# Reordering the joints of a two-layer SSD, Conformer and Fourier trunk: early products between layers, the gated norm inside the scan, and moved side work

## The chip, the cores and the metric

The kernel is one program on one core of a Trainium2 chip. The metric is the device time of one execution in microseconds (us). The kernel before takes 1757.48 us, the median of three runs (1753.33 to 1760.16).

## The reference

The program advances 640 tokens (128 of context, 512 of a noisy sample) through two layers in fp32. Layer 0 mixes tokens with a state-space scan and a convolution, layer 1 with a Fourier transform, and each layer ends in a feed-forward block with a 3x3 depthwise convolution. Before each block stands a norm that is scaled and shifted by `mod`, a product of the condition with `w_mod`. Cut to what matters:

```python
mod = silu(cond) @ w_mod[i] + b_mod[i]
sh1, sc1, gt1, sh2, sc2, gt2 = split(mod, 6)
hm = rmsnorm(x, g_mix[i]) * (1 + sc1) + sh1
if i % 2 == 0:
    proj = hm @ w_in                       # z, xbc, dt, glu
    y = ssd_scan(silu(conv5(xbc)), softplus(dt), ...)   # both directions, chunks of 128
    y_ssd = rmsnorm(y * silu(z), norm_g)   # the gated norm
    u = glu[..., :1024] * sigmoid(glu[..., 1024:])
    u = silu(layernorm(conv31(u)))
    out = concatenate([y_ssd, u]) @ w_out
else:
    out = fft2(hm by groups).real @ w + b
x = x + gt1 * out
hf = rmsnorm(x, g_ffn[i]) * (1 + sc2) + sh2
val, gate = split(conv3x3(hf @ w_up), 2)
x = x + gt2 * ((val * silu(gate)) @ w_down)
```

## The kernel before

Channels lie on the 128 partitions and the 640 tokens along the free axis, so an activation is 8 tiles of 128x640. Every large product is done as three products of fp32r halves: a weight tile `raw` arrives by SP's queue (L203), ScalarE rounds it to `wh` (L216), GpSimd subtracts to get `wl` (L219), and TensorE adds wh x xh, wh x xl and wl x xh in one accumulator (L227). The tokens are cut in two segments, in most places of 320 columns, so that a tile of eight k takes 24 matmuls for each segment.

The order on each engine is made by a scheduler of the tile framework, which places an instruction by its place in the program, the release of the buffers and the `issue_after` marks. An engine runs its queue strictly in that order, and so does SP with its DMAs.

The work comes in this order: the first norm with the `mod` columns that it needs; eight pairs of products of the convolution branch (each gives a tile of `u` at L855, a SiLU gate times a value) with `mod` vectors between them on VectorE (L268 twice and L272 for one of 128x1024); `time_steps` (L531 to L548), which makes the scan's step sizes; the projections and the scan of 4 groups by 5 chunks, with parts of products as fillers (the tables GATES, PROJ, LNAT, UFILL name the step of each); the gated norm (`y_segment`, its sums at L894 and L899, `apply` at L906 to L908); the product with `w_out`, first its u half and then its y half; feed-forward 0; the Fourier layer; feed-forward 1.

At a joint between two blocks, `by_segment` finishes the last product segment by segment: it adds to `x` (L354), collects squares (ScalarE L318, VectorE ssq L322), sums them over channels on TensorE (L329) and from this normalizes (hmt L340, xh L348, xl L349). `first_up` then starts three tiles of the next up-product together, k by k, on segment 0.

The layer norm of the convolution branch needs sums over channels. Within the convolution three GpSimd adds for each of 7 pieces make them (L631 to L633), and L950 to its neighbours apply them.

```python
UFILL = {19: 1, 20: 2, 21: 2}     # tiles of the u half as filler of the last scan steps
LNAT = (0, 1, 9, 10)              # scan steps of mean, centring, rstd, scaling
MODSP = (2, 2, 2, 2)              # mod vectors after each tile of the first projection
```

## Time and profile before

| | |
|---|---|
| Median of three runs | 1757.48 us |
| Profiled execution | 1752.11 us, span 1749.4 us |
| TensorE busy | 1642.1 us (94%) |
| VectorE busy | 1348.4 us (77%) |
| GpSimd busy | 825.4 us (47%) |
| ScalarE busy | 692.7 us (40%) |
| DMA | 189.20 MB, mean 108 GB/s |

Busy shares are means over stages with different limits. The windows of 25 us show where TensorE was full (25.00 of 25) and where it waited or ran at a lower granted clock; the list of waits says for whom it waited.

### The profile page before, as it was taken

What the parts mean: (1) busy time and instruction counts of PE and PEld (TensorE: products, weight loads), DVE (VectorE), ACT (ScalarE), POOL (GpSimd) and SP (SyncE); (2) the same over time, 40 slices, a digit from 0 to 9 for tenths busy, and PEclk for the clock granted to TensorE, in tenths of its full rate; (3) what the DMA queues carried; (4) which work ended last, traced back from release to release, by engine and by line L of the source; (5) the groups of instructions that cost most, each with busy time, mean ns of one, the idle gap of its engine ahead of it and who ended that gap; (6) DMA issues with size and microseconds to landing.
All of it is one profiled execution on the core that took longest, in us unless ns stands there. A gap on an engine that the chain in (4) does not pass through costs nothing.

```text
span 1749.4 us, 27932 instructions
## 1 busy us (share of the span) xinstructions
PE 1642.1 (94%) x10828; PEld 1576.8 (90%) x10828; DVE 1348.4 (77%) x2390; ACT 692.7 (40%) x1207; POOL 825.4 (47%) x556
## 2 busy tenths in 40 slices
PE   7989998999899879999999999889799999999997
PEld 4789987888799879999999999779799999999996
DVE  7688586878665387899999999885989838817846
ACT  4312225888763253332231232455533223313324
POOL 1233346554655353554465355404445635544544
PEclk9999998999999999999999999999999999999998
DMA  8446332332331342225324422432533232222123
GB/s 290 162 143 185 122 111 77 109 109 79 91 105 71 102 150 81 74 70 181 119 64 155 145 63 85 138 112 73 173 109 97 64 94 70 65 86 81 49 58 114
DMA packets 81911, 189.20 MB, mean 108 GB/s; under 512 B 7540, under 2 KB 33043, under 8 KB 81780
## 3 DMA queue, kind: packets, MB, share of 16 engines
q1 hardware_dynamic: 78836, 184.03, 33.7%
q10 hardware_dynamic: 2944, 3.41, 0.6%
q8 instruction: 85, 1.39, 0.3%
q14 instruction: 46, 0.38, 0.1%
HBM read 183.57 MB, written 3.83 MB: 107 GB/s over the span
## 4 chain that ended last, share of the span: by engine, by line
PE 54%; DVE 39%; issue 3%; ACT 2%; POOL 1%; DMA 1%; ACTq 0%; DVEq 0%; POOLq 0%
PE acc L227 46%; DVE cva L1039 12%; DVE mm L268 7%; DVE x L354 3%; DVE ssq L322 2%; DVE modc L272 2%; DVE cva L1028 2%; DVE hmt L340 2%; DVE mjunk L268 1%; PE misc L621 1%; PE misc L813 1%; PE misc L248 1%; PE acc L329 1%; DVE yT L906 1%; ACT sqt L318 1%
## 5 line engine op out<-in xcount | busy, mean ns | idle before, releaser
L219 POOL TENSOR_TENSOR wl<-raw,wh 128x512 fp32r<-128x512 f32 (+5 forms) x314 | 561.5, 1797 | 649.9 <-ACT wh L216 642.2
L227 PE MATMUL acc<-xh,wh 128*128 128x320 f32 (+2 forms) x2064 | 491.8, 315 | 12.1 <-DVE u L855 8.1
L1039 DVE SCALAR_TENSOR_TENSOR cva<-acc,cw,cva 128x441 f32<-128x441 f32 (+2 forms) x704 | 477.4, 691 | 16.2
L227 PE MATMUL acc<-xh,wl 128*128 128x320 f32 (+2 forms) x2064 | 485.5, 312 | 2.4 <-POOL wl L219 2.4
L227 PE MATMUL acc<-xl,wh 128*128 128x320 f32 (+2 forms) x2064 | 486.5, 313 | 0.2 <-DVE xl L349 0.2
L216 ACT CAST wh<-raw 128x512 fp32r<-128x512 f32 (+5 forms) x314 | 238.0, 768 | 576.5 <-PE acc L227 412.0
L227 PEld LDWEIGHTS acc<-xh,wh 128*128 128x128 f32 (+1 forms) x2064 | 352.6, 190 | 17.7 <-issue 14.7
L227 PEld LDWEIGHTS acc<-xl,wh 128*128 128x128 f32 (+1 forms) x2064 | 352.0, 190 | 2.4 <-issue 0.9
L227 PEld LDWEIGHTS acc<-xh,wl 128*128 128x128 f32 (+1 forms) x2064 | 350.8, 190 | 3.3 <-POOL wl L219 2.7
L354 DVE SCALAR_TENSOR_TENSOR x<-acc,modc,x 128x128 f32<-128x128 f32 (+2 forms) x240 | 112.0, 498 | 151.5 <-PE acc L227 147.0
L227 PE MATMUL acc<-fh,wh 128*128 128x320 f32 (+2 forms) x832 | 207.0, 311 | 5.3 <-DVE cva L1039 2.3
L227 PE MATMUL acc<-fh,wl 128*128 128x320 f32 (+2 forms) x832 | 206.6, 311 | 2.8 <-POOL wl L219 2.7
L227 PE MATMUL acc<-fl,wh 128*128 128x320 f32 (+2 forms) x832 | 206.2, 310 | 0.0
L227 PEld LDWEIGHTS acc<-fh,wh 128*128 128x128 f32 x832 | 143.7, 189 | 6.4 <-issue 6.0
L227 PEld LDWEIGHTS acc<-fh,wl 128*128 128x128 f32 x832 | 143.7, 189 | 4.6 <-POOL wl L219 4.2
L227 PEld LDWEIGHTS acc<-fl,wh 128*128 128x128 f32 x832 | 143.8, 189 | 0.6
L268 DVE SCALAR_TENSOR_TENSOR mm<-mm 128x1024 f32<-128x1024 f32 x72 | 126.9, 1763 | 0.8
L1067 POOL TENSOR_TENSOR cva<-cva 128x640 f32<-128x640 f32 x44 | 71.1, 1615 | 98.1 <-ACT cva L1066 98.1
L268 DVE SCALAR_TENSOR_TENSOR mjunk<-mraw,crow 128x1024 f32<-128x1024 f32 x68 | 97.7, 1437 | 6.9 <-DMA mraw<-in_w_modT 6.4
L1028 DVE SCALAR_TENSOR_TENSOR cva<-acc,cw,cva 128x127 f32<-128x127 f32 x176 | 60.0, 345 | 49.9 <-ACT cva L1024 46.2
L1071 POOL TENSOR_TENSOR fl<-cva,fh 128x640 fp32r<-128x640 f32 x44 | 70.8, 1608 | 31.8 <-ACT fh L1070 31.8
L1066 ACT ACTIVATE cva<-cva 128x640 f32<-128x640 f32 x44 | 32.4, 736 | 130.1 <-DVE cva L1039 130.1
(253 smaller groups left out, 1927.2 us busy)
## 6 DMA issues: line engine op xcount, KB each, us to landing
raw<-in_ffn_w_up SPq DMA_DIRECT2D x88, 512.0 KB, 3.7
raw<-in_w_in SPq DMA_DIRECT2D x40, 512.0 KB, 3.9
mm<-in_w_modT SPq DMA_DIRECT2D x36, 512.0 KB, 3.7
mraw<-in_w_modT SPq DMA_DIRECT2D x34, 512.0 KB, 3.8
e<-acsd SPq DMA_DIRECT2D x40, 256.0 KB, 3.4
raw<-in_ffn_w_down SPq DMA_DIRECT2D x32, 256.0 KB, 2.7
raw<-in_ffn_w_down SPq DMA_DIRECT2D x16, 448.0 KB, 3.4
raw<-in_w_out SPq DMA_DIRECT2D x24, 256.0 KB, 3.0
```

What stands on the lines that cost most here:

```text
L216: S.copy(wh[:, ks, :], raw[:, ks, :])
L219: G.tensor_tensor(wl[:, ks, :], raw[:, ks, :], wh[:, ks, :].bitcast(F32), op=SUB)
L227: PE.matmul(part(ps, s), lhsT=wt[:, k, :], rhs=tok(at, s), start=(k == 0 and p == 0), stop=(k == n - 1 and p == 2))
L268: V.scalar_tensor_tensor(junk, in0=raw[:, cs_], scalar=1.0, in1=crow[j][:, cs_], op0=MULT, op1=MULT, accum_out=m[:, 2 * o + j:2 * o + j + 1])
L272: V.tensor_scalar(modc[l][:, i, :], m[:, 0:2], b, None, op0=ADD)
L322: V.tensor_tensor(tok(self.a, s), tok(self.a, s), t, op=ADD)
L340: V.scalar_tensor_tensor(tok(t, sub), in0=tok(x[:, k, :], sub), scalar=a[:, k, j:j + 1], in1=flat(bc[:, o:o + size(sub)], sub), op0=MULT, ...
L354: last = V.scalar_tensor_tensor(tok(x[:, m, :], sub), in0=part(ps, s, o, sub), scalar=gt[:, m, j:j + 1], in1=tok(x[:, m, :], sub), op0=MUL ...
L1028: V.scalar_tensor_tensor(a[:, lo:hi], in0=ps[:, BASE + lo + d:BASE + hi + d], scalar=w(1, c), in1=a[:, lo:hi], op0=MULT, op1=ADD)
L1039: last = V.scalar_tensor_tensor(av[:, r0:r1, c0:c1], in0=pv[:, r0 + dr_:r1 + dr_, c0 + dc:c1 + dc], scalar=w(r, c), in1=av[:, r0:r1, c0:c1 ...
L1067: G.tensor_tensor(cv[0], cv[0], cv[1], op=MULT)
L1071: G.tensor_tensor(l_, cv[0], h_.bitcast(F32), op=SUB)
```

## The change

The edits, without what they are for:

1. `first_up` is split in `early(k)` and `rest`. At the joints w_out to feed-forward 0 and Fourier to feed-forward 1, the 72 matmuls of segment 0 of the next up-product are issued k by k: those of k 0 to 3 ahead of the second segment's sum of squares, those of k 4 to 7 behind it. At the joint of feed-forward 0 to the Fourier layer, `over_channels` does the same with 16 plain fp32 matmuls. Its table d1 is loaded at the front.
2. The gated norm's two segments are called inside the scan loop, after chunks 2 and 4 of the last group; `apply` stands ahead of all eight tiles of the u half, and its `yl` subtraction runs on VectorE instead of GpSimd.
3. `time_steps` is a generator in two parts, after u tiles 1 and 2, each issued behind u and tanh and ahead of the `mod` vectors.
4. The 21 GpSimd adds in the convolution become 7 adds of 128x640 at scan steps 0 and 1; the layer norm's steps move back by two.
5. Two of three groups of scale columns of the first norm are `mod` vectors on VectorE instead of TensorE products; `columns` does its transposes ahead of its adds.
6. The first three weight tiles are loaded ahead of the first `mod` loads on SP.
7. The `mod` vectors are spread anew: MODSP, MODS1, MODST, and five of them (MODSW) beside the u half of `w_out`.

```diff
-DTAT = 1
+DTAT = (1, 2)
-SCPE = (0, 3, 6)
+SCPE = (0,)
-MODSP = (2, 2, 2, 2)
+MODSP = (3, 3, 2, 0)
-LNAT = (0, 1, 9, 10)
+LNAT = (0, 2, 3, 11, 12)
-UFILL = {19: 1, 20: 2, 21: 2}
+MODSW = (1, 1, 1, 1, 1, 0, 0, 0)
-MODS1 = ({j: 1 for j in range(6)}, ((0,) * 8,) * 3)
+MODS1 = ({j: 1 for j in (0, 2, 4, 6, 7)}, ((0,) * 8,) * 3)
-MODST = (1, 0, 1, 0, 1, 0, 1, 0)
+MODST = (0,) * 8
...
             product(src, k0, acts, (s,), after)
+            if i:
+                for k in range(KD - NLAG):
+                    early(k)
             bc[i] = ss.finish(s, i * size(segs[0]))
         for k in range(KD - NLAG, KD):
             then(bc[0], segs[0], k)
+            early(k)
...
+        def early(k):
+            if k == 0:
+                ws.extend(weights(A["ffn_w_up"][l], b) for b in FIRST)
+                ps0.update((b, acc()) for b in FIRST)
+            for b, w in zip(FIRST, ws):
+                mtile_k(ps0[b], w, acts[k], k, KD, SEGS[:1])
...
+        first = [first_weights(A["w_dt"], 0), first_weights(w_in, 32), weights(w_in, 24)]
         mod_start(0)
...
+        with tc.issue_after(last.ins), tc.issue_after(tanh.ins):
+            if i in DTAT:
+                next(steps)
...
-                G.tensor_tensor(yl, y, yh.bitcast(F32), op=SUB)
+                V.tensor_tensor(yl, y, yh.bitcast(F32), op=SUB)
...
+    def ln_sum(i):
+        if i == 0:
+            L["sum"] = sm.tile([P, T], F32, tag="ssq", name="usum", bufs=1)
+        G.tensor_tensor(L["sum"], L["sum"] if i else u[:, 0, :], u[:, i + 1, :], op=ADD)
...
+            if g == 3 and c in (2, 4):
+                apply.append(y_segment(CHUNKED[c == 4]))
...
+    u_fill(len(utodo))
     for f in apply:
         f()
-    u_fill(len(utodo))
```

On TensorE, at the joint of w_out and feed-forward 0, the rows around the second segment's sum of squares (ssq, sqt against ones) and of the 16 fp32 products L1101, before (yh and yl are w_out's operands, xh and xl the next block's; 68 rows of the 72 products L227 are left out):

```order
L227 MATMUL acc<-yl,wh 128x320
L227 MATMUL acc<-yh,wl 128x320
L329 MATMUL acc<-ssq,ones 128x320
L329 MATMUL acc<-sqt,ones 128x320
L227 MATMUL acc<-xh,wh 128x320
L227 MATMUL acc<-xl,wh 128x320
...
L227 MATMUL acc<-xl,wh 128x320
L227 MATMUL acc<-xh,wl 128x320
L1101 MATMUL acc<-mraw,sc__85 2x128 x16
```

and now, around the same two matmuls:

```order
L229 MATMUL acc<-yl,wh 128x320
L229 MATMUL acc<-yh,wl 128x320
L229 MATMUL acc<-xh,wh 128x320
L229 MATMUL acc<-xl,wh 128x320
...
L229 MATMUL acc<-xl,wh 128x320
L229 MATMUL acc<-xh,wl 128x320
L331 MATMUL acc<-ssq,ones 128x320
L331 MATMUL acc<-sqt,ones 128x320
L229 MATMUL acc<-xh,wh 128x320
```

Thirty-six products of the next block now stand ahead of L331 and 36 behind it; before, all 72 stood behind L329.

On VectorE, around the third tile u (L855, now L913), the time steps (dtmp) and the `mod` vectors (mjunk), before:

```order
L540 TENSOR_TENSOR dtmp_820<-dtmp_820 128x160
L541 TENSOR_TENSOR dtmp_821<-dtmp_820 128x160
L542 TENSOR_SCALAR dtmp_821<-dtmp_821 128x160
L544 TENSOR_TENSOR dtmp_821<-dtmp_821 128x160
...
L855 SCALAR_TENSOR_TENSOR u<-sg,acc 128x128
L545 TENSOR_SCALAR dtmp_821<-dtmp_821 128x160
L855 SCALAR_TENSOR_TENSOR u<-sg,acc 128x512
```

and now:

```order
L270 SCALAR_TENSOR_TENSOR mjunk,mm<-mraw,crow_110 128x1024
L270 SCALAR_TENSOR_TENSOR mjunk,mm<-mraw,crow_111 128x1024
L274 TENSOR_SCALAR modc_88<-mm,vec 128x2
L913 SCALAR_TENSOR_TENSOR u<-sg,acc 128x128
L913 SCALAR_TENSOR_TENSOR u<-sg,acc 128x512
L603 TENSOR_SCALAR dtmp_792<-dtmp_792 128x160
L270 SCALAR_TENSOR_TENSOR mjunk,mm<-mraw,crow_110 128x1024
```

The chain of the time steps, which stood ahead of u, starts behind it.

On GpSimd, between the last weight splits of the convolution branch and the scan's first steps (usum holds the layer norm's sums, xdd and hd belong to the scan), before:

```order
L631 TENSOR_TENSOR cs<-u 128x4x67
L632 TENSOR_TENSOR cs<-cs 128x2x67
L633 TENSOR_TENSOR usum<-cs 128x67
L734 TENSOR_TENSOR xdd<-xb,dte 128x256 x7
L743 TENSOR_TENSOR hd<-h_2465,cdec 128x256
```

and now:

```order
L791 TENSOR_TENSOR xdd<-xb,dte 128x256 x2
L986 TENSOR_TENSOR usum<-usum,u 128x640
L791 TENSOR_TENSOR xdd<-xb,dte 128x256
L986 TENSOR_TENSOR usum<-usum,u 128x640
L791 TENSOR_TENSOR xdd<-xb,dte 128x256 x2
L986 TENSOR_TENSOR usum<-usum,u 128x640
L791 TENSOR_TENSOR xdd<-xb,dte 128x256
L986 TENSOR_TENSOR usum<-usum,u 128x640
L791 TENSOR_TENSOR xdd<-xb,dte 128x256
L800 TENSOR_TENSOR hd<-h_2430,cdec 128x256
```

The sums no longer stand ahead of all scan work; four of the seven adds stand among the first xdd.

## Rows read from the trace of the kernel before

**Rows 1.** The page, busy time of each engine over the span:

```profile
PE 1642.1 (94%) x10828; PEld 1576.8 (90%) x10828; DVE 1348.4 (77%) x2390; ACT 692.7 (40%) x1207; POOL 825.4 (47%) x556
```

**Rows 2.** What TensorE waited for: total us, times, longest us:

```profile
PE acc L329 <- DVE ssq L322: 25.7, 8, 7.5
PE acc L227 <- DVE x L354: 8.5, 2, 6.3
PE acc L227 <- DVE u L855: 8.1, 1, 8.1
...
PE acc L227 <- DVE cva L1039: 4.5, 4, 2.3
...
PE misc L717 <- ACT xb L719: 3.7, 1, 3.7
```

**Rows 3.** Windows: stretch, length, PE, PEld, DVE, ACT, POOL busy, granted clock, DMA:

```profile
725.00:750.00 25.00, 25.00 (x172) 25.00 (x171) 23.09 (x39) 8.05 (x10) 14.88 (x8) 1.00 0.22 62
1125.00:1150.00 25.00, 17.67 (x107) 13.46 (x107) 22.78 (x63) 14.03 (x28) 7.31 (x9) 0.86 0.69 236
1250.00:1275.00 25.00, 22.32 (x138) 19.97 (x139) 18.21 (x36) 12.41 (x23) 4.83 (x2) 0.86 0.49 170
1325.00:1350.00 25.00, 24.77 (x168) 24.53 (x167) 25.00 (x41) 8.04 (x11) 16.91 (x8) 1.00 0.31 90
```

**Rows 4.** Timeline at the front: start us, us, engine, line, names [idle before]:

```profile
19.10 8.08 POOL L219 TENSOR_TENSOR wl<-raw,wh 128x128 fp32r<-128x128 f32 x6 [18.66 <-ACT wh L216]
...
21.09 2.28 DVE L268 SCALAR_TENSOR_TENSOR mjunk<-rawv,crow 128x1024 f32<-128x1024 f32 x1
...
27.38 0.22 PE L255 MATMUL acc<-con,mrow 2*128 2x2 f32 x1 [3.17 <-DVE modc L256]
...
31.09 1.22 DVE L268 SCALAR_TENSOR_TENSOR mjunk<-rawv,crow 128x1024 f32<-128x1024 f32 x1
```

**Rows 5.** The chain of waits at the front, a group of mod columns on TensorE:

```profile
40.52 1.84 PE misc L248 x16
```

**Rows 6.** Timeline around u tile 2, TensorE:

```profile
99.77 0.46 PE L227 MATMUL acc<-xh,wl 128*128 128x320 f32 x2
...
113.71 0.87 PE L227 MATMUL acc<-xh,wh 128*128 128x320 f32 x2 [8.13 <-DVE u L855]
114.38 0.74 PE L227 MATMUL acc<-xl,wh 128*128 128x320 f32 x2
```

**Rows 7.** Timeline at the scan's start, ScalarE:

```profile
273.55 2.01 ACT L719 COPY xb<-misc 128x384 f32<-128x384 f32 x5 [7.40 <-POOL usum L633]
```

**Rows 8.** The page's costliest groups, a GpSimd add of 128x640: busy, mean ns, idle before:

```profile
L1067 POOL TENSOR_TENSOR cva<-cva 128x640 f32<-128x640 f32 x44 | 71.1, 1615 | 98.1 <-ACT cva L1066 98.1
```

**Rows 9.** Timeline of the gated norm on VectorE and TensorE:

```profile
518.89 1.01 DVE L896 TENSOR_TENSOR yT<-yT,gz 128x384 f32<-128x384 f32 x2
...
548.60 0.81 PE L894 MATMUL misc<-yss,ones 128*128 128x384 f32 x2
...
554.95 0.61 DVE L906 SCALAR_TENSOR_TENSOR yT<-yT,vec,yss 128x384 f32<-128x384 f32 x1
...
557.96 13.44 DVE L906 SCALAR_TENSOR_TENSOR yT<-yT,vec,yss 128x384 f32<-128x384 f32 x13
...
572.46 0.87 PE L227 MATMUL acc<-uh,wh 128*128 128x320 f32 x2 [6.31 <-DVE x L354]
```

**Rows 10.** The line L908 on GpSimd, ns min/median/max, first and last start:

```profile
L908 POOL TENSOR_TENSOR yl<-yT,yh x16: 740/1056/1389, 555.1 to 573.3; 128x384 fp32r<-128x384 f32 x8, 128x256 fp32r<-128x256 f32 x8
```

**Rows 11.** Timeline of the joints at 642 to 655 and 1250 us, GpSimd, then TensorE:

```profile
648.99 4.90 POOL L219 TENSOR_TENSOR wl<-raw,wh 128x1024 fp32r<-128x1024 f32 x2 [3.46 <-ACT wh L216]
...
651.74 1.44 PE L329 MATMUL acc<-ssq,ones 128*128 128x320 f32 x2 [7.52 <-DVE ssq L322]
...
1252.68 1.43 PE L329 MATMUL acc<-ssq,ones 128*128 128x320 f32 x2 [7.54 <-DVE ssq L322]
```

**Rows 12.** Windows of 5 us after the wait at 651.74 us, columns as in rows 3:

```profile
650.00:655.00 5.00, 3.26 (x8) 2.47 (x9) 5.00 (x6) 1.99 (x5) 3.90 (x2) 0.50 0.46 118
```

More of the change, by code (lines that the diff above doesn't have):

```diff
@@ L185, in _body @@
     V.memset(eps, EPS)
+    d1 = one.tile([P, 4 * P], F32, name="d1")
     def big_tile(dt, name, n=T):
@@ new lines, in mods_between @@
+    def mods_between(n):
+        if not n:
+            return
+        ps = acc()
+        ws = [todo.pop(0) for _ in range(n)]
+        for i, (l, w) in enumerate(ws):
+            raw = wp.tile([P, KD, P], F32, tag="raw", name="mraw", bufs=RAWB)
+            nc.sync.dma_start(raw, A["w_mod"][l][w])
+            for k in range(KD):
+                PE.matmul(ps[0:2, P * i:P * i + P], lhsT=sc_[:, k, :], rhs=raw[:, k, :], start=(k == 0), stop=(k == KD - 1))
+        mr = sm.tile([P, 384], F32, tag="sqt", name="mrow", bufs=3)[0:2, 0:P * n]
+        S.copy(mr, ps[0:2, 0:P * n])
+        for i, (l, w) in enumerate(ws):
+            PE.transpose(ps[:, 512 + 2 * i:514 + 2 * i], mr[:, P * i:P * i + P], ident[0:2, 0:2])
+            V.tensor_scalar(modc[l][:, w, :], ps[:, 512 + 2 * i:514 + 2 * i], vc("b_mod", 48 * l + w), None, op0=ADD)
@@ new lines, in _body, with __init__, __call__ @@
+    class Background:
+        def __init__(self, rows, junk, raws):
+            self.crow, self.junk, self.raws, self.n = rows, junk, raws, 0
+            for j in range(2):
+                nc.sync.dma_start(rows[j], A["condr"][:, D * j:D * j + D].broadcast_to([P, D]))
+                S.activation(rows[j], rows[j], AF.Silu)
+        def __call__(self, ins, n):
+            with tc.issue_after(ins.ins):
+                for l, i in [todo.pop(0) for _ in range(min(n, len(todo)))]:
+                    mod_vector(self.raws(), self.junk, self.crow, l, i)
@@ L404, in _body, with big_background @@
+    def big_background():
+        mm = x_tile("mm").rearrange("p k t -> p (k t)").rearrange("p (i d) -> p i d", d=D)
+        n = iter(range(100))
+        return Background([mm[:, j, :] for j in range(2)], mm[:, 2, :], lambda: mm[:, 3 + next(n) % 2, :])
     w_in = A["w_in"]
@@ L487, in _body @@
         norm_tile(0)
-        first = [(acc()[0:32, :], first_weights(A["w_dt"], 0)), (acc(), first_weights(w_in, 32)), (acc(), weights(w_in, 24))]
+        first = [(acc()[0:n, :], w) for n, w in zip((32, P, P), first)]
         for k in range(KD):
@@ L583, in _body @@
         V.memset(ut[:, :, o:o + n], 0.0)
-    usum = sm.tile([P, T], F32, tag="ssq", name="usum", bufs=1)
     def outputs(b):
@@ L927, in ln_mean @@
         for s in SEGS:
-            PE.matmul(part(ps, s), lhsT=ones, rhs=tok(usum, s), start=True, stop=True)
+            PE.matmul(part(ps, s), lhsT=ones, rhs=tok(L["sum"], s), start=True, stop=True)
         S.mul(L["mu"], ps[:, BASE:BASE + T], 1.0 / D)
@@ L1002, in _body, with ffn @@
     xh, xl, then = ffn_norm(0, x)
[L1003 removed]
+    early, rest = first_up(0, xh, xl)
+    transition(A["w_out"], 0, acts_of(Y["h"], Y["l"]), x, after_w, gt, then, early)
     yp_.__exit__(None, None, None)
[L1007 to L1008 removed]
+    def ffn(l, x, xh, xl, background, mods, rest, segs, then, early=None):
         mods_up, mods_down = mods
@@ L1170, in _body @@
         V.tensor_tensor(gb, gt1, vs("fnet_b", 0, KD)[:, :, None].broadcast_to([P, KD, 2]), op=MULT)
-        vp = big_tile(F32, "vp")
-        for g in range(KD):
-            ps = misc()
-            PE.matmul(ps[:, 0:256], lhsT=f[:, g, 0:P], rhs=d1[:, 0:256], start=True, stop=True)
-            PE.matmul(ps[:, 256:512], lhsT=f[:, g, 4 * P:5 * P], rhs=d1[:, P:P + 256], start=True, stop=True)
-            S.copy(vp[:, g, 0:512], ps)
+        vp = F["vp"]
         fh = x_tile("fh", F32R)
@@ L1225, in _body @@
         xh, xl, then = ffn_norm(1, x)
+        early, rest = first_up(1, xh, xl)
         def after(m, ps):
@@ L1230, in after @@
                 S.activation(x[:, m, c0:c0 + cn], x[:, m, c0:c0 + cn], AF.Identity, bias=gb[:, m, j:j + 1])
-        transition(A["fnet_w"], 0, acts_of(fh, fl), x, after, gt1, then)
+        transition(A["fnet_w"], 0, acts_of(fh, fl), x, after, gt1, then, early)
     def final(bc, s, k):
```

117 lines of the change are left out of this document (42 added, 75 removed).

## The prediction

> **What bounds the kernel now.** I read the busy shares first: TensorE is busy for 94% of the span, 1642.1 of 1749.4 us, VectorE for 77% [rows 1]. So at most 107 us are idle on TensorE, and a change that removes no TensorE work can win only there and where its clock is low. Next I read the windows. Most of the program looks like 725 to 750 us: TensorE 25.00 of 25, 172 matmuls, clock 1.00 [rows 3]. One matmul of 320 columns thus takes 25/172 = 0.145 us there. The joints look otherwise: at 1125 to 1150 us TensorE is busy for 17.67 us and VectorE for 22.78; at 1250 to 1275 the clock is 0.86 [rows 3]. Then I read for whom TensorE waits: 25.7 us for the squares ssq of the joints, 8.5 for x, 8.1 for u in one piece, 4.5 for cva, 3.7 for xb [rows 2]. These five sums are 50.5 us, nearly half of the idle time, and each stands at a place that the change touches. Last I read the timelines there; behind each long wait the reader sees a half clock: after u, a pair of matmuls takes 0.74 us where it took 0.46 before [rows 6], and the window 650 to 655 has clock 0.50, the lower level of 1.2 GHz [rows 12].
>
> **The change, part by part.** The sum is made against the profiled execution, 1752.11 us with 2.7 us around its span. The median of the runs is 1757.48, so 5.4 us are added at the end.
>
> *Front (parts 5 and 6).* Weight splits on GpSimd run from 19.10 to 27.18 us [rows 4], just when VectorE makes the first mod vector: a pass takes 2.28 us there and 1.22 later, and TensorE waits 3.17 us for the first columns [rows 4]. With weights ahead of the mod loads the splits start earlier, beside squares, and the 3.17 us should mostly go. Against it stand 1.2 MB (one tile of 128x256 and two of 128x1024 in fp32) that are queued ahead of the mod loads on SP. Two groups of columns at 1.84 us on TensorE [rows 5] go; two mod vectors of 2 x 1.22 us plus a short add, about 2.6 us each, come to VectorE [rows 4]. Once the weights are in, VectorE, not TensorE, is late next, because it makes every normed tile here. I take a gain of 3.0; bounds: nothing (VectorE's 5.2 us eat it all) to 5 (3.17 plus one of the two groups).
>
> *Time steps (part 3).* TensorE waits 8.13 us for u tile 2, behind the arithmetic of the step sizes, and restarts at half clock [rows 6]. The restart costs (0.74 - 0.46) a pair over some five pairs, 1.4 us. Now u stands ahead of that arithmetic, as the VectorE rows of the new order show. Tile 2 still has three mod vectors ahead of it, and the steps move beside the next pairs of products, each of which has 2 x 48 = 96 matmuls of 0.145 us, 13.9 us, for VectorE to work beside. I take 7.5 of the 9.5 us; bounds 6 (a mod vector of 2.6 us and its neighbours stay in the way) to 9.5.
>
> *Layer norm sums (part 4).* ScalarE waits 7.40 us on usum before it makes xb [rows 7], and TensorE 3.7 on xb [rows 2]. The new order takes the sums out of that way, so the 3.7 go and some of the half clock that follows. Four of the seven adds stand among the first xdd on GpSimd: 4 x 1.615 = 6.5 us [rows 8], and hd, on which the recurrence rests, queues behind them. Forty-three products are behind the first group of steps as cover, 6.2 us. I take a gain of 3.0; bounds: a loss of 3 (6.5 less the 3.7) to a gain of 6 (3.7 and the half clock).
> This is where a rule speaks against the change. The trace shows a VectorE pass at 2.28 us beside splits and 1.22 without, 1.06 longer, less than one split of 8.08/6 = 1.35 us [rows 4]: it lost part of the time that GpSimd was busy. The Trainium skill, "SBUF — State Buffer", section "Terms", says that the port pair shared by VectorE and GpSimd is locked for the whole instruction and the loser fully blocks. By this rule the four adds would stop VectorE for 6.5 us among the scan's first steps, the term would be 3.0 - 6.5 = -3.5, and the sum 6.5 us longer. By the row, the share is 1.06 of 2.28, 3.0 us, and much of that is idle time of VectorE. I go by the row; the last 6.5 us are in the second rival.
>
> *Gated norm (part 2).* TensorE waits 6.31 us for x at 572 us, because thirteen passes of L906 fill 13.44 us, 1.03 each beside GpSimd's subtractions, and 0.61 where they are alone [rows 9, 10]; x and the accumulators queue behind them. Its input was ready early: the last gating multiply ended at 519.9 and the sums started on TensorE at 548.60 [rows 9], 28.7 us of slack. Now apply stands ahead of the whole u half, eight tiles of 48 matmuls, 56 us. The 16 subtractions that come to VectorE cost at most 16 x 0.61 = 9.8 us, less 13 x 0.42 = 5.5 us that no longer contend, and lie beside these 56 us; if that cover were gone they would cost 4.3. TensorE's sums for the norm now have little other work ahead of them and may stop it for about 3 us. So 6.31 and 1.5 of half clock less 3: I take 5.0; bounds 2 to 8.
>
> *Joints w_out and Fourier to the feed-forward (part 1).* The waits are 7.52 and 7.54 us [rows 11]. Thirty-six matmuls take 36 x 0.145 = 5.2 us, and they now stand in front of each. Their operands of segment 0 are normed by VectorE before that time, but the third of their weight tiles is split by GpSimd only at 648.99 + 4.90 = 653.9 us, after TensorE's L329 started at 651.74 [rows 11]. So part of the 36 is late and holds back the sums behind it by up to 2.2 us. On VectorE, which is busy throughout (5.00 of 5 in the window [rows 12]), nothing goes, so what follows the joint may wait instead. I take 4.0 a joint, 8.0; bounds 0 and 16 (the whole wait and a restart at full clock).
>
> *Feed-forward 0 to Fourier.* The remaining part of the 25.7 us is 25.7 - 15.06 = 10.6 for six waits, and VectorE is the fuller engine (22.78 of 25 [rows 3]). Sixteen fp32 products go into the wait, but the stage ends when VectorE has made the last f. I take 2.0; bounds 0 and 4.
>
> *Mod vectors spread anew (part 7).* In feed-forward 1 VectorE has 25.00 of 25 and TensorE waits 4.5 us for cva [rows 2, 3]. One vector of six leaves, and fewer come before the products that could cover them: 3.0, bounds 0 and 4.5. The five beside w_out lie beside TensorE's tiles of 24 x 0.145 = 3.5 us and take at least 2.6 each with the residual behind them, which four accumulators can absorb; four leave the Fourier stage. I take these two as nothing, bounds -5 (five times a slowed vector, 2 x 2.28 us, less the tile's 3.5 that cover it) and 3.
>
> Sum: 3.0 + 7.5 + 3.0 + 5.0 + 8.0 + 2.0 + 3.0 = 31.5. 1752.1 - 31.5 = 1720.6, and 5.4 more give 1726 as a median. The likeliest case's own range is 1715 to 1737.
>
> **The rivals.**
> *The early products block.* They wait for the third weight tile, the sum of squares behind them comes later, and the norm of segment 1 starts as late as before. For it: the 653.9 against 651.74 [rows 11] and a VectorE without a gap. Against it: the first two tiles are ready before. Both joints and the Fourier joint then give nothing: 1726 + 10 = 1736.
> *The sums choke the scan's start.* Part 4 loses 3.5 rather than winning 3, and contention adds some 3: 1726 + 6.5 + 3 = about 1736. For it: GpSimd's adds stand ahead of hd; against it: the 43 products of cover.
> *The gated norm stops TensorE: the slower one.* In the new order 240 fewer products stand ahead of its first sum, 240 x 0.145 = 34.8 us, more than the slack of 28.7. If the scan's last y came as late as that, the queue of TensorE would stand until then at three places, with all the u half behind. Its price is up to 34.8 and three restarts of 1.5, 39 us: 1765. It decides from about 31 us on. Against it: in the trace y was ready 28.7 us early, so most of the loss would have to come from a slower scan.
> *Waits only move.* VectorE's 1348.4 us stay and each hole opens at its next product: 1755. Against it: VectorE has 400 us free, and u and x are plain reorderings.
> *All at the good end.* Both joints lose nearly the whole wait and the scan runs smoother: front 5, steps 9, sums 5, norm 7, joints 13, the rest 8, together 47: 1710.
>
> **How the numbers follow.** Forecast 0.37; early products block 0.20; sums choke 0.13; waits only move 0.08; slower 0.07; good end 0.15. The range of 8 in 10 goes from the good end's lower side, 1703, to 1748, above both middle rivals, and leaves out the last two bad ones with part of the good end. About 0.5% (8.8 us) can be told from no change. Faster by more than that: forecast, good end, both middle rivals, 0.85; within it: waits only move and half of an unlucky sum, 0.09; slower: 0.06.
>
> **What would show each step.** The wait for u at 113 us gone and no 0.74 us pairs behind it; xb no longer behind usum; apply finished before the y half starts; at both joints early products in place of the 7.5 us wait, the sum of squares within 3 us of its old distance from the squares, clock 1.00; in feed-forward 1 less than 2 us on cva. The prediction is wrong if TensorE's busy time, which falls here only by the front's 3.7 us and the restarts, stays while its idle time does not fall by some 25 us, or if a new wait of over 5 us stands in the scan, at the norm's sums or behind an early product.

## The result, and the profile after

The changed kernel takes 1728.3 us, the median of four runs (1726.67 to 1728.85), against 1756.93 for the kernel before (four runs, 1753.33 to 1760.16): a ratio of 0.9836, 95% interval 0.9815 to 0.9857. The medians differ by 28.6 us. In the profiled executions the span fell from 1749.4 to 1727.1 us, by 22.3; there is one such execution of each kernel, and before's (1752.11) is faster than each of the four runs above, while after's is the slowest of its four. All stretches below are compared by spans and by points in the two traces.

The page's row of busy times, which answers to [rows 1]:

```profile
PE 1636.6 (95%) x10794; PEld 1570.9 (91%) x10794; DVE 1358.5 (79%) x2398; ACT 698.2 (40%) x1211; POOL 804.9 (47%) x526
```

TensorE is busy for 5.5 us less and idle for 90.5 instead of 107.3 us, 16.8 less. VectorE has 10.1 us more. The list of TensorE's waits answers to [rows 2] (total us, times, longest us):

```profile
PE acc L229 <- POOL wl L221: 10.7, 12, 1.9
PE acc L229 <- ACT wh L218: 8.3, 4, 2.4
PE acc L1228 <- ACT v L1216: 7.1, 2, 5.8
PE misc L848 <- DVE hn L801: 7.1, 6, 3.0
PE acc L229 <- ACT xh L350: 5.6, 3, 4.7
PE misc L793 <- POOL xdd L791: 5.3, 6, 1.5
PE acc L331 <- DVE ssq L324: 5.1, 5, 2.4
PE acc L634 <- DVE u L913: 4.9, 1, 4.9
...
PE acc L229 <- DVE x L356: 2.2, 1, 2.2
...
PE acc L229 <- DVE u L913: 1.1, 1, 1.1
```

The waits that were aimed at are gone or small: ssq 5.1 for 25.7, x 2.2 for 8.5, u in the gate's place 1.1 for 8.1; cva and xb no longer stand in the list. Others have come: for weights at the joints (wl and wh), for v in the Fourier layer, for xh at the front, and for u at L634, the scan's tables. In the scan the waits for xdd grew from 3.5 to 5.3 us and those for hn from 6.2 (4.1 and 2.1 at two lines) to 7.1.

To see where the time came from, I set the start of the same instruction in both traces side by side.

| point of the program | before | after | gain so far |
|---|---|---|---|
| first u | 70.57 | 70.14 | 0.4 |
| u tile 2 | 112.53 | 102.19 | 10.3 |
| u tile 3 | 129.69 | 123.76 | 5.9 |
| last u | 206.15 | 201.67 | 4.5 |
| first y of the scan (L835, L892) | 307.0 | 296.7 | 10.3 |
| first product of the y half of w_out | 583.35 | 565.35 | 18.0 |
| end of the w_out joint (L1101, L440 end) | 669.29 | 649.48 | 19.8 |
| first sum of the Fourier joint | 1117.83 | 1098.13 | 19.7 |
| first dfts product (L1209, L1228) | 1158.03 | 1140.17 | 17.9 |
| first sum of the Fourier to feed-forward 1 joint | 1227.69 | 1212.14 | 15.6 |
| end of the Fourier to feed-forward 1 joint | 1270.25 | 1253.28 | 17.0 |
| last cva of L1028, L1093 | 1670.7 | 1648.3 | 22.4 |

The scan with the gated norm and feed-forward 1 give most. Tile 2 gains ten microseconds and loses six of them within three tiles, and the Fourier layer costs some four.

The timelines of after show why (start us, us, engine, line, names, and idle time before in brackets). First the front, answering to [rows 4, 5]:

```profile
55.20 1.14 ACT L218 CAST wh<-raw 128x512 fp32r<-128x512 f32 x2 [7.13 <-DMA raw<-in_w_in]
56.24 1.01 ACT L350 ACTIVATE xh<-hmt,modc 128x128 fp32r<-128x128 f32 x2
57.31 1.81 PE L229 MATMUL acc<-xh,wh 128*32 128x320 f32 x6 [4.71 <-ACT xh L350]
```

ScalarE stands for 7.13 us in front of a cast whose transfer lands at 55 us, and xh, whose input VectorE finished at 50.76 us, stands behind it in the queue. TensorE waits 4.71 us for that xh. Then the time steps, answering to [rows 6]:

```profile
102.19 0.89 DVE L913 SCALAR_TENSOR_TENSOR u<-sg,acc 128x128 f32<-128x128 f32 x2 [1.51 <-PE acc L229]
103.22 0.53 PE L229 MATMUL acc<-xh,wh 128*128 128x320 f32 x2 [1.14 <-DVE u L913]
...
141.22 2.31 PE L634 MATMUL acc<-con,la 128*32 128x128 f32 x10 [4.93 <-DVE u L913]
```

The wait of 8.13 us is 1.14 now, at full clock, but 38 us later L634 waits 4.93 us. Third, TensorE at the joint of w_out and feed-forward 0, answering to [rows 11]:

```profile
627.61 0.41 PE L229 MATMUL acc<-xh,wl 128*128 128x320 f32 x1 [1.09 <-POOL wl L221]
630.35 0.63 PE L229 MATMUL acc<-xh,wh 128*128 128x320 f32 x1 [2.33 <-ACT wh L218]
...
632.80 0.64 PE L229 MATMUL acc<-xh,wl 128*128 128x320 f32 x1 [1.55 <-POOL wl L221]
...
639.37 0.70 PE L331 MATMUL acc<-ssq,ones 128*128 128x320 f32 x2
```

The early products start at 626.07 and L331 begins at 639.37: 13.3 us for products worth 36 x 0.145 = 5.2. They wait 4.97 us for weights, and the window of 5 us answering to [rows 12] shows what follows those waits (PE, PEld, DVE, ACT, POOL busy, clock, DMA):

```profile
630.00:635.00 5.00, 3.10 (x10) 2.70 (x11) 4.96 (x4) 2.25 (x5) 4.62 (x2) 0.52 0.28 84
```

The granted clock is at the lower of its two levels again, 0.52, and VectorE still has no gap (4.96 of 5). But it is not working all that time. Rows of GpSimd, VectorE and ScalarE from the same timeline, in order of time:

```profile
624.91 2.65 POOL L221 TENSOR_TENSOR wl<-raw,wh 128x1024 fp32r<-128x1024 f32 x1 [0.46 <-ACT wh L218]
625.25 2.45 DVE L342 SCALAR_TENSOR_TENSOR hmt<-x,A,bc 128x128 f32<-128x128 f32 x1
628.25 0.47 ACT L320 ACTIVATE sqt<-x 128x320 f32<-128x320 f32 x1 [3.42 <-DVE x L356]
629.27 1.03 ACT L218 CAST wh<-raw 128x1024 fp32r<-128x1024 f32 x1
...
632.82 2.65 DVE L324 TENSOR_TENSOR ssq<-ssq,sqt 128x320 f32<-128x320 f32 x1
...
636.88 0.35 DVE L342 SCALAR_TENSOR_TENSOR hmt<-x,A,bc 128x128 f32<-128x128 f32 x1
```

The same hmt takes 0.35 us alone and 2.45 beside a weight split, and it ends 0.14 us after the split does. Behind it come x (627.62), on ScalarE the square of x and only then the cast of the next weight tile, for which TensorE waits the 2.33 us. The ssq at 632.82 is held up in the same way (2.65 us; 0.48 alone, as at 629.00), and so is before's last ssq ahead of the 7.52 us wait, beside the split of [rows 11]:

```profile
649.49 2.20 DVE L322 TENSOR_TENSOR ssq<-ssq,sqt 128x320 f32<-128x320 f32 x1
```

So a part of the joints' wait is VectorE standing still for GpSimd's splits. The rows show this; no run moved the splits away, so what that would give is not shown.

### The profile page after: what moved, and what is told of

It reads as the page before. It is cut to its first block, busy times and chain, and to the rows that moved or that the text cites. A ratio compares the mean times of both kernels' runs of the same rounds, so it can differ in the third digit from the quotient of the medians.

```text
span 1727.1 us, 27861 instructions
## 1 busy us (share of the span) xinstructions
PE 1636.6 (95%) x10794; PEld 1570.9 (91%) x10794; DVE 1358.5 (79%) x2398; ACT 698.2 (40%) x1211; POOL 804.9 (47%) x526
## 4 chain that ended last, share of the span: by engine, by line
PE 43%; DVE 22%; issue 3%; ACT 2%; POOL 1%; DMA 0%; DVEq 0%; POOLq 0%; ACTq 0%
PE acc L229 40%; DVE cva L1104 8%; DVE mm L270 6%; DVE x L356 2%; DVE modc L274 1%; DVE cva L1093 1%; DVE ssq L324 1%; POOL wl L221 1%; PE acc L331 1%; PE acc L440 1%; ACT sqt L320 1%; DVE x L1261 1%; PE acc L1228 0%; DVE hmt L342 0%; ACT fh L1235 0%
## 5 line engine op out<-in xcount | busy, mean ns | idle before, releaser
L1104 DVE SCALAR_TENSOR_TENSOR cva<-acc,cw,cva 128x504 f32<-128x504 f32 (+2 forms) x704 | 479.2, 692 | 16.6
L270 DVE SCALAR_TENSOR_TENSOR mm<-mm 128x1024 f32<-128x1024 f32 x80 | 138.1, 1726 | 1.2 <-DMA mm<-in_w_modT 0.2
L1093 DVE SCALAR_TENSOR_TENSOR cva<-acc,cw,cva 128x127 f32<-128x127 f32 x176 | 61.0, 346 | 49.3 <-ACT cva L1089 44.2
## 6 DMA issues: line engine op xcount, KB each, us to landing
raw<-in_ffn_w_up SPq DMA_DIRECT2D x88, 512.0 KB, 3.6
raw<-in_w_in SPq DMA_DIRECT2D x40, 512.0 KB, 3.7
mm<-in_w_modT SPq DMA_DIRECT2D x40, 512.0 KB, 3.6
mraw<-in_w_modT SPq DMA_DIRECT2D x34, 512.0 KB, 3.7
```

The lines of the kernel that those rows point to most:

```text
L270: V.scalar_tensor_tensor(junk, in0=raw[:, cs_], scalar=1.0, in1=crow[j][:, cs_], op0=MULT, op1=MULT, accum_out=m[:, 2 * o + j:2 * o + j + 1])
L1093: V.scalar_tensor_tensor(a[:, lo:hi], in0=ps[:, BASE + lo + d:BASE + hi + d], scalar=w(1, c), in1=a[:, lo:hi], op0=MULT, op1=ADD)
L1104: last = V.scalar_tensor_tensor(av[:, r0:r1, c0:c1], in0=pv[:, r0 + dr_:r1 + dr_, c0 + dc:c1 + dc], scalar=w(r, c), in1=av[:, r0:r1, c0:c1 ...
```

## The experiments

Each is an edit of the changed kernel, timed in three rounds beside the kernel before. "After" is the changed kernel (span 1727.1); spans are of the profiled execution. I held that each part pays where its wait stood, with VectorE as what is late next; the rival, for each part, was that its wait only moves or that something new blocks.

A span is one execution, and it carries what that execution did elsewhere. From the first sum of the Fourier joint to the end of the joint behind it, after takes 155.15 us (1098.13 to 1253.28), and four kernels that change nothing there (casts_behind_norm, undo_steps, mods_later, undo_gated) take 152.6 to 152.8. In after the clock falls to 0.84 in a stretch where it stays at 1.00 in mods_later (first after, then mods_later):

```profile
1115.00:1120.00 5.00, 2.86 (x8) 1.81 (x9) 5.00 (x14) 2.93 (x7) 1.80 (x5) 0.84 0.85 244
```

```profile
1115.00:1120.00 5.00, 3.23 (x13) 2.28 (x14) 5.00 (x16) 3.45 (x9) 1.35 (x3) 1.00 0.91 260
```

The first u, too, comes between 68.0 and 70.1 us in kernels that are alike up to there. So differences of spans under about 3 us say little, and I give the time of the stretch that an edit changes beside them.

**undo_first_up.** All 72 products of the two joints behind the sum again.

```diff
-        by_segment(src, k0 + n, acts[n:], x, gt, SEGS, then, early)
+        by_segment(src, k0 + n, acts[n:], x, gt, SEGS, then)
+        for k in range(KD):
+            early(k)
```

> The changed kernel with the 72 early products of both w_out-like joints put back behind the norms; everything else as changed. In the changed trace the joints gained only 1.9 and 1.3 us. Theory (VectorE bounds the joints, the early products only move TensorE's idle time): the wait for ssq of about 7.5 us is back at both joints, each joint is 1 to 3 us longer, the whole 3 us slower than the changed kernel, about 1731. Rival (early products were worth the whole wait of 7.5 us each and something else took it back): about 15 us slower, 1743. Rival (they cost something because they hold back the sum of squares): 0 to 3 us faster.

1731.59 us, ratio 0.9861 (0.9845 to 0.9878), span 1730.0: 2.9 us over after, for both joints together. Its waits and the sum at the first joint:

```profile
PE acc L331 <- DVE ssq L324: 20.2, 7, 7.5
...
PE acc L229 <- POOL wl L221: 5.1, 8, 1.1
```

```profile
634.28 1.44 PE L331 MATMUL acc<-ssq,ones 128*128 128x320 f32 x2 [7.52 <-DVE ssq L324]
```

The wait of 7.52 us is back, to the hundredth that of [rows 11], while waits for weights halve. From the first product of the y half to the end of the joint it takes 86.16 us against 84.12 in after, and at the second joint 42.49 against 41.14. So the early products are right and worth 2.0 and 1.4 us, not 4 each: most of the wait was exchanged for waits on weights.

**joint_halves.** The three weight tiles of a joint rounded and split in pieces of 2 k, so that the first pieces come earlier.

```diff
             if k == 0:
+                whole = list(grain)
+                grain[:] = 2, 2
                 ws.extend(weights(A["ffn_w_up"][l], b) for b in FIRST)
+                grain[:] = whole
```

> The changed kernel with the three weight tiles of the early products rounded and split in halves, so that k 0 to 3 need only the first halves. At the joint the 36 early products take 12.9 us where their own time is 5.3, with waits of 1.1, 2.3 and 1.6 us on weights, and the sum of squares starts 5.6 us later than before against the end of the last product. Theory (the weights hold them back): the sum of squares starts 1.5 to 3 us earlier, each joint is 1 to 2 us shorter, the whole 2 to 4 us faster, 1725. Rival (VectorE bounds the joint): the sum starts earlier, VectorE's wait of 1.26 us behind it shrinks, and the whole changes by under 1.5 us.

1727.9 us, 0.9823 (0.9795 to 0.9851), span 1727.3: no change. L331 starts at 642.01, 15.6 us behind the last wait of the y half on weights (626.38); in after these are 639.37 and 624.50, 14.9 us. The waits, wl then wh, in its list:

```profile
PE acc L229 <- ACT wh L218: 11.3, 6, 2.4
...
PE acc L229 <- POOL wl L221: 6.9, 10, 1.1
```

Wl falls from 10.7 to 6.9 and wh rises from 8.3 to 11.3. Smaller pieces move the wait from the split to the cast; the sum is not earlier, which neither theory had.

**undo_over_channels.** The 16 fp32 products at feed-forward 0 to Fourier behind the sums again.

```diff
-    ffn(0, x, xh, xl, background, MODS0, rest, RUNS, fourier_norm, over_channels)
+    ffn(0, x, xh, xl, background, MODS0, rest, RUNS, fourier_norm)
+    for g in range(KD):
+        over_channels(g)
```

> The changed kernel with the 16 fp32 products over channels put back behind the whole norm of the Fourier layer. The Fourier stage lost 4 us against the kernel before: VectorE waits 3.49 us for two mod columns whose 16 products now start behind the early ones. Theory (the early products pushed the mod columns back, and VectorE bounds the stage): without them the columns are made in TensorE's wait again, VectorE's wait of 3.49 us is gone or under 1.5, the stage as before the change, the whole 2 to 5 us faster than the changed kernel, 1724. Rival (the early products are worth 2 us as forecast, and the loss has another cause): 2 us slower, 1730, with the wait of 3.49 still there.

1725.38 us, 0.9827 (0.9812 to 0.9842), span 1723.3: 3.8 us faster than after, 1.3 of them already ahead of the first sum of this joint. In this place the change costs time, though the wait of 5.48 us for ssq that it took away is back here. The rows of the mod columns (L445, VectorE), in after and then here:

```profile
1130.12 0.22 DVE L445 TENSOR_SCALAR modc<-acc,vec 128x2 f32<-128x2 f32 x1 [3.49 <-PE acc L444]
...
1140.17 3.78 PE L1228 MATMUL acc<-dfts,v 128*128 128x128 f32 x16 [5.84 <-ACT v L1216]
```

```profile
1127.24 0.22 DVE L445 TENSOR_SCALAR modc<-acc,vec 128x2 f32<-128x2 f32 x1 [0.34 <-PE acc L444]
```

In after VectorE stands idle for 3.49 us at the column, with the arithmetic of f and hmt queued behind it; here for 0.34. TensorE makes the columns from L440's products (L1101 before; 16 in the program, 32 records in the trace). In after these stand as one block at 1125.70, behind the early products; here the first 18 are at 1117.32, between the norm's two sums. In the four kernels named above, which keep after's order, the idle time at the column is 2.42 to 2.44 us: about one of the 3.49 belongs to after's low clock.

**fourier_mods_early.** The early products kept, but the mod columns called ahead of the joint's last tiles.

```diff
-        elif k == 0:
+        elif s == RUNS[0] and k == KD - NLAG:
             mods_between(MODSB[1])
```

> The changed kernel with the two mod columns of the Fourier joint issued ahead of the second half of the early products instead of behind them. Theory (position of the columns alone is the loss): VectorE's wait of 3.49 us falls below 1, TensorE's wait of 5.84 us for v shrinks by about 3, the whole 3 to 4 us faster, 1725. Rival (the columns are on TensorE's path anyway): the time moves elsewhere in the stage, no change.

1724.58 us, 0.982 (0.9805 to 0.9835), span 1723.4: 3.7 us faster than after, as much as taking the early products away. The column waits 0.16 us, and the sine products start earlier, behind a wait for v of 4.34 us in place of 5.84 (a fall of about 3 was expected):

```profile
1126.84 0.22 DVE L445 TENSOR_SCALAR modc<-acc,vec 128x2 f32<-128x2 f32 x1 [0.16 <-PE acc L444]
```

```profile
1136.92 3.78 PE L1228 MATMUL acc<-dfts,v 128*128 128x128 f32 x16 [4.34 <-ACT v L1216]
```

From the first sum to the first dfts product it takes 38.95 us; the eight traced kernels that keep after's order take 40.96 to 42.06, undo_over_channels 40.30. So the cost was the order of the columns. The early products themselves give about 1 us at most here: from the first sum to the end of the second joint 151.48 us against undo_over_channels' 152.42, with spans that differ by 0.1.

**casts_behind_norm.** The weights of the convolution branch are called behind the first norm's last xh.

```diff
+            with tc.issue_after(last_xh[0].ins):
+                w = weights(w_in, 32 + i)
-            mtile(pg, weights(w_in, 32 + i), acts, GAPPED)
+            mtile(pg, w, acts, GAPPED)
...
```

> The changed kernel with ScalarE's rounding of the next weight tiles queued behind the last normed tile of the front. In the changed trace ScalarE waits 7.13 us at 55 us for a weight transfer, TensorE 4.71 us for xh behind it and runs at half clock after. Theory (ScalarE's queue order put a transfer in front of the norm): the wait of 4.71 us is gone, the first u tile is 4 to 6 us earlier than at 70.1; of this 2 to 5 us stay to the end, since VectorE is full at u tiles 2 to 4: 1724 to 1726. Rival (VectorE bounds the front, with its two added mod vectors): the first u tile stays within 1.5 us of 70.1, no change.

1721.49 us, 0.9806 (0.979 to 0.9823), span 1718.3: 8.8 us under after by span, 6.8 by median.

```profile
57.35 2.17 ACT L218 CAST wh<-raw 128x512 fp32r<-128x512 f32 x4
...
63.02 0.89 DVE L919 SCALAR_TENSOR_TENSOR u<-sg,acc 128x128 f32<-128x128 f32 x2 [4.21 <-ACT sg L911]
```

The casts now stand behind xh and wait for nothing, and the first u comes at 63.02 instead of 70.14. More of it stays than I expected (2 to 5 us): 6.7 us at the last u and 6.3 at the y half; VectorE, which is late in the tiles that follow, begins earlier too. The rest up to 8.8 lies in the Fourier layer, which the edit does not touch. The cause is ScalarE's queue.

**undo_steps.** The time steps in one piece again, ahead of the next u.

```diff
-        with tc.issue_after(last.ins), tc.issue_after(tanh.ins):
-            if i in DTAT:
-                next(steps)
...
+        if i == 1:
+            list(steps)
```

> The changed kernel with the time steps back in one piece behind u tile 1, as before the change. Between u tiles 2 and 5 the change gained 5 us net: 8.1 us of TensorE's wait at u tile 2 went, 4.9 us for u tile 4 came. Theory (VectorE's work of this stretch is its bound, so that the long wait is only partly won): the 8 us wait at tile 2 is back, the 4.9 us wait is gone or small, 3 to 6 us slower than the changed kernel, 1733. Rival (the full 7.5 us of the forecast are in this part, and the other wait has nothing to do with it): 7 to 9 us slower, 1736, with both waits in the trace.

1728.83 us, 0.9865 (0.9843 to 0.9887), span 1727.6: the same as after within 0.5 us, by span and by median.

```profile
111.20 0.87 PE L229 MATMUL acc<-xh,wh 128*128 128x320 f32 x2 [8.21 <-DVE u L913]
```

The 8.21 us are back, and the 4.9 us at L634 are gone from its list. The 0.5 is too low a price, because this run's Fourier layer is 2.4 us shorter than after's: from the second u, behind which the edit begins, to the last u it takes 115.45 us against 114.33, and to the y half 1.6 us more than after. By the ratios, against a before that ran at 1751.46 us in this batch, it could be up to 5. The stretch is mostly VectorE's: it is busy for 23.28 and 24.04 us in the windows 100 to 125 and 125 to 150 of after. A wait there moves more than it vanishes: 8.2 us of wait are worth 1 to 2, and my size for this part, both readings on record included, was too large.

**mods_later.** The same work spread otherwise: two mod vectors leave tiles 2 and 3 for tiles 6 and 7.

```diff
-MODSG = (3, 3, 4, 4, 3, 3, 3, 3)
+MODSG = (3, 3, 3, 3, 3, 3, 4, 4)
```

> The changed kernel with one mod vector each taken from u tiles 2 and 3 and given to u tiles 6 and 7, where VectorE idles over 8 us ahead of each u. Theory (VectorE's queue, too full at tiles 2 to 4, makes the wait of 4.9 us): that wait falls below 1.5 us, 3 to 5 us faster than the changed kernel, 1724. Rival (the wait comes from the two accumulators alone and not from VectorE's load): no change.

1726.73 us, 0.9853 (0.9827 to 0.9879), span 1724.2: 2.9 us under after by span and 1.6 by median, where 3 to 5 were expected. L634 starts at 134.97 without a wait, 6.3 us earlier, and the last u comes at 193.96 instead of 201.67. But the first repeated wait for xdd at the scan's start comes only 3.9 us earlier (264.27 against 268.13), and the first product of the y half 0.7 us earlier (564.64 against 565.35). Waits for yT and xb (2.4 and 1.4 us; in after 1.0 and none) stand in its list instead. So the tiles u are relieved and the scan gives nearly all of it back; the rest of the 2.9 us lies in the Fourier layer, which the edit does not touch.

**undo_sums.** The layer norm's sums in the convolution again, with the early steps of before.

```diff
-LNAT = (0, 2, 3, 11, 12)
+LNAT = (0, 0, 1, 9, 10)
...
+                G.tensor_tensor(t, u[:, 0:4, cs], u[:, 4:8, cs], op=ADD)
+                G.tensor_tensor(t[:, 0:2, :], t[:, 0:2, :], t[:, 2:4, :], op=ADD)
+                G.tensor_tensor(usum[:, cs], t[:, 0, :], t[:, 1, :], op=ADD)
...
-        fillers[LNAT[0] + i // 4].append(lambda i=i: ln_sum(i))
```

> The changed kernel with the layer norm's sums back in the convolution on GpSimd and its steps at their old places. Theory (the sums stood between TensorE and the scan, and the four adds among the first xdd cost less than the products behind them cover): TensorE's wait of 3.7 us at the scan's start and the half clock after it are back, 4 to 6 us slower, 1733. Rival (the adds choke the scan's start): 0 to 3 us faster than the changed kernel.

1733.48 us, 0.9898 (0.9871 to 0.9926), span 1730.5: 3.4 us slower than after (5.2 by median), where 4 to 6 were expected. The wait for cvb is 3.7 us in this list and not in after's:

```profile
PE misc L783 <- ACT cvb L756: 3.7, 2, 2.9
```

Part 4 is worth 3.4 us by span and 4.0 from the last u to the first y (99.02 against 95.03), near the 3.0 of the sum. The rival, the adds stopping the scan's start, is seen only in part: TensorE waits 5.3 us for xdd with the adds among them and 4.2 here. By the Trainium skill's "SBUF — State Buffer", section "Terms", the loser of the port pair shared by VectorE and GpSimd fully blocks. The traces agree, at the joint (hmt 2.45 us beside a split, 0.35 alone) and here: two of VectorE's e (L841), 0.35 us each in the median, take 2.15 us at 272.41 in after, beside an add from 272.80 to 274.41. It costs little because VectorE has room there, 5.44 us of work between 264.0 and 275.6.

**undo_gated.** The gated norm behind the scan again, with the u half as filler and `yl` on GpSimd.

```diff
+UFILL = {19: 1, 20: 2, 21: 2}
...
-                V.tensor_tensor(yl, y, yh.bitcast(F32), op=SUB)
+                G.tensor_tensor(yl, y, yh.bitcast(F32), op=SUB)
...
-            if g == 3 and c in (2, 4):
-                apply.append(y_segment(CHUNKED[c == 4]))
...
+    for s in CHUNKED:
+        apply.append(y_segment(s))
...
-    u_fill(len(utodo))
     for f in apply:
         f()
+    u_fill(len(utodo))
```

> The changed kernel with the gated norm behind the scan loop, three u-half tiles as filler of its last steps, and the subtraction on GpSimd, as before the change. Theory (the norm's sums had 28.7 us of slack, so that nothing is paid for asking for them early): the wait of about 6 us for x and the half clock behind it are back, 7 to 10 us slower, 1737. Rival (the forecast's: early sums cost about 3 us, so that 5 net are lost by undoing it): 1733.

1738.28 us, 0.9916 (0.9892 to 0.994), span 1735.6: 8.5 us slower than after (10.0 by median).

```profile
565.85 0.87 PE L230 MATMUL acc<-uh,wh 128*128 128x320 f32 x2 [6.31 <-DVE x L357]
```

The wait of [rows 9] is back to the hundredth. The part is worth 8.5 us by span, and 8.7 from the first y to the y half (277.31 us against 268.65). The run undoes the place of the norm, the fillers and the engine of `yl` together; which of them gives how much is not shown.

**undo_mods1.** Feed-forward 1's six mod vectors as before, four beside w_out.

```diff
-MODSW = (1, 1, 1, 1, 1, 0, 0, 0)
+MODSW = (1, 1, 1, 1, 0, 0, 0, 0)
-MODS1 = ({j: 1 for j in (0, 2, 4, 6, 7)}, ((0,) * 8,) * 3)
+MODS1 = ({j: 1 for j in range(6)}, ((0,) * 8,) * 3)
```

> The changed kernel with feed-forward 1's mod vectors at their old places (six, at up tiles 0 to 5) and four instead of five beside the u half of w_out. In the changed trace feed-forward 1 is 5 us shorter and TensorE's wait of 4.5 us for cva is gone. Theory (VectorE is full in the first up tiles there, and each vector in them is time): the waits for cva return with 3 to 5 us in sum, 3 to 6 us slower, 1733; beside w_out nothing moves. Rival (the gain there comes from the joint before it): no change, 1728.

1734.59 us, 0.9862 (0.9832 to 0.9892), span 1734.2: 7.1 us slower than after (6.3 by median; 3 to 6 were expected), 7.0 of them between the end of the second joint and the last cva. Its wait list and two of its windows (columns as above):

```profile
PE acc L229 <- DVE cva L1104: 4.5, 4, 2.3
```

```profile
1325.00:1350.00 25.00, 23.97 (x163) 23.73 (x163) 25.00 (x44) 7.06 (x9) 14.94 (x7) 1.00 0.28 85
1350.00:1375.00 25.00, 21.74 (x137) 21.27 (x136) 22.86 (x42) 7.42 (x10) 12.83 (x7) 0.93 0.18 53
```

The 4.5 us for cva are back; TensorE, which is full in both windows in after (25.00 at clock 1.00), loses 1.0 and 3.3 us, and the second falls to clock 0.93. The wait alone is less than the part.

**combined.** casts_behind_norm, mods_later and fourier_mods_early in one kernel.

```diff
-MODSG = (3, 3, 4, 4, 3, 3, 3, 3)
+MODSG = (3, 3, 3, 3, 3, 3, 4, 4)
...
+            with tc.issue_after(last_xh[0].ins):
+                w = weights(w_in, 32 + i)
...
-        elif k == 0:
+        elif s == RUNS[0] and k == KD - NLAG:
```

> The changed kernel with three edits together: ScalarE's casts behind the last normed tile of the front, mod vectors later among the u tiles, and the Fourier joint's mod columns ahead of the second half of its early products. Theory (three separate places, of which the first two touch the same VectorE-bound stretch): alone they gave about 7, 2 to 3 and 4 us; together 12 to 14, 1715. Rival (the first two win the same time): 10 to 11, 1718.

1716.11 us (1715.34 to 1717.96), 0.9758 (0.9727 to 0.9789), span 1716.2: 10.9 us under after by span, 12.2 by median, and faster than both kernels. The three gave 8.8 + 2.9 + 3.7 = 15.4 alone by span and 6.8 + 1.6 + 3.7 = 12.1 by median. So the 4.5 us between 15.4 and 10.9 are not time that two of the edits share: the spans of casts_behind_norm and mods_later hold 2.5 and 2.4 us of Fourier layer that neither edit changes. By points this kernel is 7.7 us ahead of after at the first u, 7.7 at the y half and 10.8 at the end of the second joint: the first and the third edit stay whole, and of mods_later nothing is left.

**combined_one_ahead.** combined, with only k 0 of the early products ahead of the sum at the two joints.

```diff
             if i:
-                for k in range(KD - NLAG):
+                for k in range(ahead):
                     early(k)
             bc[i] = ss.finish(s, i * size(segs[0]))
+        for k in range(ahead, KD - NLAG):
+            early(k)
```

> The combined kernel with only k 0 of the early products (9 instead of 36 matmuls) ahead of the sum of squares at the two joints, the others behind it. Theory (the number of early products ahead of the sum decides between an idle TensorE and a late sum, and neither is far from the other, because VectorE's norms end the joint): the sum starts 2 to 4 us earlier, VectorE's wait for it (1.3 us) goes, TensorE waits 2 to 4 us for the squares instead, and the whole changes by under 2 us from the 1716 of the combined kernel. Rival (the late sum is what keeps the joints from gaining the forecast 4 us each): 3 to 6 us faster, 1711.

1721.62 us, 0.9801 (0.9779 to 0.9824), span 1720.3: 4.1 us slower than combined, 5.5 by median. Neither reading on record has that: one held a change under 2 us, the other a gain. The sum and the first of the 32 matmuls that end the joint, of combined and then of this kernel:

```profile
631.91 0.70 PE L331 MATMUL acc<-ssq,ones 128*128 128x320 f32 x2
...
638.36 3.65 PE L442 MATMUL acc<-mraw,sc__86 128*2 128x128 f32 x32
```

```profile
628.24 1.44 PE L331 MATMUL acc<-ssq,ones 128*128 128x320 f32 x2 [1.48 <-DVE x L358]
...
641.52 3.65 PE L444 MATMUL acc<-mraw,sc__86 128*2 128x128 f32 x32
```

The sum comes 3.7 us earlier and the joint ends 3.2 us later; the second joint takes 2.3 us longer too (43.57 against 41.26). So the late sum is not what limits the joints: TensorE's own products end them, and with 27 of them moved out of the wait the end comes later.

## Why the prediction was near, and which steps failed

The forecast of 1726 lies 2.3 us under the measured 1728.3. How far the sum of 31.5 was off depends on what it is held against: the medians fell by 28.6 us, the spans of the profiled executions, on which it was made, by 22.3, 9 less. Of the 32 other runs of before only 5 are faster than the profiled 1752.11, so the 5.4 us added for the median were fair; but the sum's terms were read in that one execution, and what they are worth in the others no trace shows. That the forecast is near is luck in part: by the last column of the table, or by points for the front, three terms were 1.0 to 4.0 us too small and four were 2.6 to 6.4 too large.

| term | forecast | by points of the two traces | by experiment, span | by experiment, in its stretch |
|---|---|---|---|---|
| front | 3.0 | 0.4 | not undone | not undone |
| time steps | 7.5 | 4.1 to the last u, with other parts | 0.5 | 1.1 |
| layer norm sums | 3.0 | 5.8 to the first y | 3.4 | 4.0 |
| gated norm | 5.0 | 7.7 with the rest of the scan | 8.5 | 8.7 |
| joints w_out and Fourier | 8.0 | 1.8 at the first, 1.4 at the second | 2.9 | 3.4 |
| feed-forward 0 to Fourier | 2.0 | -1.8 to dfts, -4.1 to the next joint | -3.8 | -2.7 |
| mod vectors | 3.0 | 5.4 in feed-forward 1 | 7.1 | 7.0 |

The spans of the experiments add up to 18.6 of 22.3 us, the stretches to 21.5. Of the 4.1 us by points to the last u, 3.1 lie between the first and the second u, ahead of the time steps; before takes 20.3 us there, after 17.2, and undo_gated, which changes nothing there, 20.2.

*Front: failed.* The step "the 3.17 us should mostly go" was answered by ScalarE's queue, which the prediction did not look at: with weights loaded early, casts of the next tiles come to stand ahead of xh and wait for a DMA. casts_behind_norm shows that as the cause.

*Time steps: failed in size.* The wait went as forecast, "beside the next pairs of products" VectorE did make the steps, but with three and four mod vectors a tile it had little free time for them, and L634 waited in u's stead. "Waits only move" was right for most of this part.

*Layer norm sums: right.* Xb no longer waits, and the adds cost the scan about 1 us of waits for xdd. The reading that VectorE loses only a share beside GpSimd (1.06 of 2.28 us) was wrong: 1.06 us is also the rest of a split that a blocked pass waits out, and the rows at the joint show whole splits waited out. The adds were cheap because VectorE had room, as the last half-sentence of that reading says.

*Gated norm: right, too small.* The 3 us taken off because TensorE's sums "may stop it" did not occur. The groups of after between 505 and 560 us (busy, mean ns, then idle time before them) show no idle time at the second segment's sums L953 and L958, and the first segment's, at 500.11 and 503.35 us, have none either:

```profile
L958 PE MATMUL misc<-sqt,ones 128*128 128x256 f32 x4 | 1.1, 405 | 0.0
...
L953 PE MATMUL misc<-yss,ones 128*128 128x256 f32 x2 | 0.6, 378 | 0.0
```

Two sentences on the order were wrong, point 2 of the list of edits and the one in the prediction: in the program text the u half stands ahead of `apply`, and only the sums are called earlier. The scheduler placed `apply` early all the same (L965 runs from 512.0 to 534.3 us, 31 before the y half starts at 565.35), so the mechanism held. The slower rival, a stop of TensorE at the norm, was not seen.

*Joints: half the mechanism.* "Part of the 36 is late" was right but far too small: 2.2 us forecast, 13.3 us for 5.2 of products measured. That the sum comes later was right too, but of no cost (combined_one_ahead). What limits the gain is the weights' own way through ScalarE and GpSimd. "VectorE, which is busy throughout" was read from its busy time alone: several passes there stand still for most of a split, and that is on the way of the squares and of the weights' casts.

*Feed-forward 0 to Fourier: wrong in sign.* The step "sixteen fp32 products go into the wait" forgot what stood right behind that wait, the small matmuls of the mod columns, on which VectorE's norm waits. That is a moved instruction that was not followed past the others in its queue.

*Mod vectors: right, too small.* The term took 3.0 of the 4.5 us of cva; with all of the waits and the half clock behind them it was 7.1. Beside w_out the fifth vector cost nothing, as taken.

Of the signs that the prediction named, the u wait, xb, `apply` and cva came out as said. At the w_out joint the sum stands 3.9 us behind the squares (635.47 to 639.37), not within 3, and at clock 0.52, not 1.00. Two of its signs of being wrong are there in part: the idle time fell by 16.8 us and not by some 25, while the busy time fell by 5.5; and a wait of 5.84 us, for v, stands behind the early products of the Fourier layer.

## What to carry to other kernels

Two waits of TensorE here were worth very different times, and the load of the engine that ended them goes with it: the 8.2 us of undo_steps, with VectorE busy for 23.67 of the 25 us around them, were worth 1 to 2 us, the 6.3 us of undo_gated, with VectorE busy for 12.55 of the next 25, 8.7. A full engine in a window need not be working: compare a pass with its own time elsewhere (2.45 and 0.35 us for one hmt). Before work is put into a hole, read what stands in it or behind it on the same engine now, and who waits for that. An early load brings its cast along, and on ScalarE, which worked in the order of its queue, a cast that waited 7.13 us for a DMA held back an xh that was ready. And before the spans of single executions are added or subtracted, compare a stretch that no edit touches: here it moved by 2.5 us.
